# Three changes to the order of work in a two-block transformer kernel on one core: next weights in two parts around the norm's rows, first tile's rows between the second tile's heads, last unit's up product in one part

## Chip, cores and metric

One core of a Trainium2 chip runs the whole program. The metric is the device time of one execution in microseconds (us). In the tables PE is the matrix engine (PEld its weight loads), DVE the vector engine, ACT the scalar engine, POOL the GpSimd engine and SP the engine that issues most of the transfers (DMAs).

## What is computed

Two blocks of two layers each, on 256 tokens of width 1024 in fp32. The first block (token mixers and dense feed-forward layers) is not touched. Each layer of the second block is, in the reference:

```python
def second_block(x, positions, w_in, ..., expert_w_down, ln2_g, ln2_b):
    ...
    for l in range(DEPTH):                     # 2 layers
        mix = hybrid_mixer(x, tabs, w_in[l], mla_q_norm[l], mla_kv_norm[l], mla_w_uq[l], mla_w_ukv[l], w_o[l])
        x = layer_norm(DEEPNORM_ALPHA * x + mix, ln1_g[l], ln1_b[l])
        moe = hier_moe(x, router_group_w[l], ..., expert_w_gate[l], expert_w_up[l], expert_w_down[l])
        x = layer_norm(DEEPNORM_ALPHA * x + moe, ln2_g[l], ln2_b[l])
    return x
```

`hybrid_mixer` projects x by `w_in` into the inputs of three kinds of attention (the last is a dilated-window attention with four heads) and projects their outputs by `w_o`. `hier_moe` picks for each token a group of experts and two experts of its eight; there are 32 experts, each with `silu(x Wg) * (x Wu)` of width 256 and a product with `Wd`.

## The kernel before

The tokens are two tiles, t = 0 and 1, of 128 rows. A scheduler fixes one instruction order for each engine ahead of time; `tc.issue_after` and `tc.keep_in_program_order` steer it. An engine works through its own order, so an instruction that waits holds up all behind it. An fp32 product is three matmuls (`mm3`, L186): weights and data are each split into a high part, cast by ACT (`whi`, `x`, `yh`), and a low part, subtracted by DVE or POOL (`wlo`, `yl`).

**Splitting weights.** `raw_w` (L148) issues the load of a 4-chunk block into one of three `raw` buffers; `split_raw` (L158) casts it on ACT (L165) and subtracts on a given engine (L166), in four pieces. The mixer's first three projections of `w_in` have 416, 384 and 296 columns; the first has its weights loaded and split ahead, under the end of the layer before (`ahead`).

**Dilated heads, norm, router** (end of `mix2`, L950 on). `dil_pair` (L886) does scores on PE, the masked minimum on DVE (L901), exponentials on ACT (L906), scaling on DVE (`shares`, L650), transposes and the product with v on PE, then the split of the result (`x<-po`). Two pairs make one tile. `out_proj` (L945) multiplies by `w_o`; `rt.logits` (L1023) adds the residual (`raw`, L1027) and makes the router's logits; LayerNorm statistics follow; `rt.route` and `rt.place` pick experts and slots. `lows` (L1052) are the two low parts of a tile's normalised rows, 128x512 each. `nrm.affine` (L690, operations at L694) multiplies h by the norm's weight row and adds its bias row: four 128x512 operations a tile, eight in all. They come last, just ahead of the branch. The two rows lie in a buffer `rowb`, which is then loaded with expert weights.

**MoE.** The 32 experts go in eight units of four, 32 slots of tokens to an expert. `load` (L1175) issues 1 MB weight loads on SP into a ring of buffers. `gate_up` (L1235) does the gate product of a unit, then a branch on the token count (`most_i`, L1380 to L1386), then the up product; in the last unit (`parts=2`) the up product of its first three experts first, and of the fourth after it. DVE multiplies (`hq`, L1262), `hidden` transposes, `down` (L1272) multiplies by the down weights in column cuts, each split to `yh` (ACT, L244) and `yl` (DVE, L245); `spread` (L1295) sends the slots back to tokens.

**Between the layers.** `finish` (L1305) runs the last unit and then `nrm.finish` (L696): statistics, a square root by Newton steps on DVE (L258 to L272), two operations per half tile (L707, L708), after each of which `then` (L1474) transposes the new half for the next layer and splits it. Two weight blocks of the next layer (four chunks of 416 columns each) are split while this goes on, on POOL; so is the projection of 384 columns (`proj`, L767).

Of the kernel before, what the change touches and what calls it, by code (L numbers as in the profile page):

```python
# [8 lines left out]
F32 = mybir.dt.float32  # L9
# [8 lines left out]
NT = 2  # L18
# [9 lines left out]
CAP, NU = 32, NE // 4  # L28
MORE = 3
PIECES = 4  # L30

SPIN = 9

# [70 lines left out]
def tile_fn(ctx: ExitStack, tc: tile.TileContext, a: dict, out: bass.AP, stop=None, start=1):  # L104
# [538 lines left out]
    def exps(X, nm, sums):  # L643
        for t, (c0, c1) in enumerate(SPAN):
            nc.scalar.activation(X[:, c0:c1], X[:, c0:c1], AF.Exp, scale=-1.0, bias=nm[:, t:t + 1], accum_out=sums[:, t:t + 1])

    def shares(X, rs, PT):

        for r, c0, c1 in rs:
            nc.vector.tensor_scalar(X[:, c0:c1], X[:, c0:c1], r, None, op0=OP.mult)  # L650
        pt = ps.tile([128, 4, 128], F32, name="tp", tag="at", bufs=PB["at"])
        for b in range(3):
            nc.tensor.transpose(pt[:, b], X[:, b * 128:(b + 1) * 128], ident)
        PT = PT().rearrange("p (b c) -> p b c", b=3)
        nc.scalar.copy(PT, pt[:, :3])
        return PT
# [57 lines left out]
    def mix2(l, xp, wx, x, last, tabs, rt, ahead):  # L714
# [49 lines left out]
            kpe.append(kp)  # L764

        with tc.issue_after(last.ins) if last else nullcontext():
            acc = proj(x, w, 416, 384, eng=nc.gpsimd)  # L767
        for t in range(NT):
            kk = t384("bqk")
            nc.scalar.copy(kk[:, :320], acc[t][:, :320])  # L770
# [179 lines left out]
        nrm = LayerNorm("ln1", a["ln1_g_2"][l:l + 1, :], a["ln1_b_2"][l:l + 1, :])  # L950
        for t in range(NT):
            pair = [dil_pair(t, n) for n in range(2)]
            for n in (0, 1, 0, 1) if t == 0 else (0, 0, 1, 1):
                next(pair[n])
            for k in (0, 2, 4):
                for c in range(2):
                    out_proj(t, c, range(k, k + 2))
            if t:

                for low in lows:  # L960
                    low()
                rt.place(0)
            for c in range(2):
                out_proj(t, c, range(6, 8))
            raw = rt.logits(t, [acc[t, c] for c in range(2)])
            with tc.issue_after(rt.copied.ins):
                for c in range(2):
                    nrm.stat(t, c, raw[c])
            mv, y = nrm.stats(t)
            nb = nrm.shift(mv, y)  # L970
            with tc.issue_after(nrm.shifted.ins):
                rt.route(t, mv, y)

            lows = rt.features(t, raw, y, nb)
            if t == 0:
                rt.gates(t)
            else:
                lows[0]()
                rt.place(t)
                lows[1]()  # L980

        def affine():
            for t in range(NT):
                for c in range(2):
                    nrm.affine(t, c, nc.vector)
        return lambda: rt.gates(1), affine

    NR = 40

    class Route:  # L990
# [68 lines left out]
        def evacuate(self, xe, pg, k0, n):  # L1059

            for k in range(n):
                g, b = self.gx[:, 0, k0 + k:k0 + k + 1], self.gx[:, 1, k0 + k:k0 + k + 1]
                if k % 2:
                    nc.vector.tensor_scalar(xe[:, k0 + k], pg[:, k], g, b, op0=OP.mult, op1=OP.add)
                else:
                    nc.scalar.activation(xe[:, k0 + k], pg[:, k], AF.Identity, scale=g, bias=b)

# [94 lines left out]
    def moe(l, xp, wx, rt, then, ahead, rest):  # L1162
# [69 lines left out]
                for e, r in experts[i]:  # L1232
                    nc.vector.tensor_copy(gs[r, q:q + 1], pq[r, q, e:e + 1])

        def gate_up(i, xe, gs, between=None, after=None, parts=1, room=None):  # L1235

            units = list(enumerate(experts[i]))

            def product(m, us, pu):
                for k in range(8):  # L1240
                    for u, (_, r) in us:
                        nc.tensor.matmul(pu[r], xe[:, k, r], W[i][4 * m + u][:, k], start=k == 0, stop=k == 7, skip_group_check=True)  # L1242

            def new_pu():
                return ps.tile([128, 512], F32, name="at", tag="at", bufs=PB["at"])[:, :EH]
            hh, hq = room or (None, None)
            pu = new_pu()
            product(0, units, pu)
            if hh is None:
                hh = xp.tile([128, EH], F32, name="hh", tag="hh", bufs=1)  # L1250
            nc.scalar.activation(hh, pu, AF.Silu)
            if between:
                between()
            pu = new_pu()
            for us in (units,) if parts == 1 else (units[:3], units[3:]):
                product(1, us, pu)
            if after:
                after()
            if hq is None:
                hq = xp.tile([128, EH], F32, name="hq", tag="hq", bufs=1)  # L1260
            hq = hq.rearrange("s (k p) -> s k p", k=2)
            nc.vector.scalar_tensor_tensor(hq.rearrange("s k p -> s p k"), hh.rearrange("s (p k) -> s p k", k=2), gs,  # L1262
                                           pu.rearrange("s (p k) -> s p k", k=2), op0=OP.mult, op1=OP.mult)
            return hq
# [40 lines left out]
        def finish(i, PT, xe, gs, nrm, most):  # L1305

            acc = {}

            def start(c):

                for t in range(NT):
                    acc[t, c] = new_acc()
                    nc.tensor.matmul(acc[t, c], ident, h[t][:, c * 512:(c + 1) * 512], start=True, stop=False, skip_group_check=True)  # L1313
            hq = gate_up(i, xe, gs, lambda: rounds(i, most, CAP), lambda: start(0), parts=2)
            for n, (sl, y) in enumerate(down(i, hidden(hq), "at", cuts)):
                c, w = divmod(sl.start, 512)
                if n == 0:
                    start(1)
                for t in range(NT):
                    p = acc[t, c][:, w:w + sl.stop - sl.start]  # L1320
                    spread(p, PT, t, y, False)
                    nrm.stat(t, n, p)
            with tc.issue_after(done[0].ins):
                for k0 in ahead:
                    ahead[k0] = split_raw(ahead[k0], 4, 416, nc.gpsimd)
            nrm.finish([[acc[t, c] for c in range(2)] for t in range(NT)], then, l + 1 == DEPTH)

        def further(i, off):
# [43 lines left out]
        for i in range(NU):  # L1372
# [23 lines left out]
                finish(i, PT[:, q], xq, gq, nrm, most)  # L1396
            load(12 * (i + 1) + NB)
            if i == NU - 2:
                if l + 1 < DEPTH:
                    for k0 in (0, 4):  # L1400
                        ahead[k0] = raw_w(*block_w(a["w_in_2"][l + 1], k0, 4, 0, 416))
                nrm = LayerNorm("ln2", a["ln2_g_2"][l:l + 1, :], a["ln2_b_2"][l:l + 1, :], len(cuts), True)

    def store():
        for t in range(NT):
# [53 lines left out]
    for l in range(DEPTH):  # L1459
# [14 lines left out]
        def then(t, c):  # L1474
            sl = slice(c * 512, (c + 1) * 512)
            if l + 1 == DEPTH or stop == f"moe{l}":
                nc.sync.dma_start(out[0, t * 128:(t + 1) * 128, sl], h[t][:, sl])
            else:
                if c == 0:
                    nxt[t] = new_x(t)  # L1480
                r = split_t(h[t][:, sl], nxt[t], 4 * c, 4)
                if t == 0:
                    last.append(r)
        nxt, ahead = [None] * NT, {}
        with tc.tile_pool(name=f"moe{l}", bufs=1) as xp:
            moe(l, xp, wx, rt, then, ahead, rest)
# [32 lines left out]
```

## Time and profile before

| | |
|---|---|
| median of 3 runs | 1698.84 us (1697.95 to 1699.92) |
| the profiled execution | 1697.12 us |
| its span, first to last instruction | 1695.3 us |
| PE busy | 1560.3 us, 92% |
| DVE / ACT / POOL busy | 54% / 40% / 3% |
| mean granted PE clock | 0.952 of full speed |

The profiled execution is 1.7 us below the median and 1.8 us above its own span. The page shows busy shares over the whole span. Within it the dense parts keep PE busy without a gap, and the two MoE stretches (about 1050 to 1250 us and 1466 to 1672 us) keep the DMA engines busy at 414 to 419 GB/s while PE waits now and then.

### The profile page before, as it was taken

To read this page: it belongs to the slowest core of one execution; us is meant where nothing else is said; L and a number is where in the kernel's file an instruction comes from. 1 tells how busy PE (TensorE), PEld (TensorE's weight loads), DVE (VectorE), ACT (ScalarE), POOL (GpSimd) and SP (SyncE) were. 2 spreads that over 40 slices of the span, in tenths; PEclk is the share of its full clock that TensorE was granted. 3 is DMA by queue.
4 is the path that set the end of the run, shared out by engine and by line. 5 is a ranking of instruction groups with operands and counts; after the bars stand their busy time and mean duration, and the time that the engine had idled before them with its cause. 6 is when DMAs were issued, how large, how long until landed. Compare 5 with 4: busy or idle time off the path is not lost. (4 is left out here: it accounts for less than half of the span.)

```text
span 1695.3 us, 24281 instructions
## 1 busy us (share of the span) xinstructions
PE 1560.3 (92%) x9488; PEld 1183.4 (70%) x9488; DVE 909.1 (54%) x1990; ACT 679.5 (40%) x1118; POOL 58.2 (3%) x86
## 2 busy tenths in 40 slices
PE   9999999999999999999999998786679999877686
PEld 7788888888878888888887776442338777544353
DVE  6757576544675767555378656331147955522133
ACT  6543454443554345444356653110116655211011
POOL 0000000000000000000110100000011010000000
PEclk9999999999999999999999999897789999898699
DMA  9354555465635454646452728999985473899994
GB/s 326 125 176 163 172 198 194 154 200 197 210 124 174 154 192 153 198 161 211 155 162 78 286 108 318 419 418 419 418 311 162 130 259 134 332 418 418 419 415 164
DMA packets 133985, 399.36 MB, mean 236 GB/s; under 512 B 8133, under 2 KB 36805, under 8 KB 110278
## 3 DMA queue, kind: packets, MB, share of 16 engines
q1 hardware_dynamic: 130096, 390.62, 62.7%
q10 hardware_dynamic: 3734, 6.69, 1.1%
q8 instruction: 95, 1.56, 0.4%
q14 instruction: 60, 0.49, 0.1%
HBM read 396.24 MB, written 1.05 MB: 234 GB/s over the span
## 5 line engine op out<-in xcount | busy, mean ns | idle before, releaser
L166 DVE TENSOR_TENSOR wlo<-raw,whi 128x2048 fp32r<-128x2048 f32 (+6 forms) x314 | 405.8, 1310 | 305.2 <-ACT whi L165 304.6
L165 ACT CAST whi<-raw 128x2048 fp32r<-128x2048 f32 (+7 forms) x346 | 354.9, 1063 | 325.5 <-PE acc L192 273.8
L190 PE MATMUL acc<-whi,x 128*128 128x512 f32 (+3 forms) x1248 | 481.7, 387 | 0.1
L191 PE MATMUL acc<-wlo,x 128*128 128x512 f32 (+3 forms) x1248 | 477.2, 383 | 0.0
L192 PE MATMUL acc<-whi,x 128*128 128x512 f32 (+3 forms) x1248 | 476.3, 382 | 0.1
L190 PEld LDWEIGHTS acc<-whi,x 128*128 128x128 f32 x1248 | 236.9, 190 | 44.7 <-issue 3.5
L191 PEld LDWEIGHTS acc<-wlo,x 128*128 128x128 f32 x1248 | 237.0, 190 | 42.7 <-issue 2.7
L192 PEld LDWEIGHTS acc<-whi,x 128*128 128x128 f32 x1248 | 236.5, 190 | 42.5 <-issue 1.4
L1242 PE MATMUL at<-whi,xe 128*32 128x256 f32 x448 | 101.1, 434 | 21.3 <-DMA whi<-in_expert_w_gate_dram 15.0
L1242 PE MATMUL at<-wlo,xe 128*32 128x256 f32 x416 | 85.7, 442 | 17.4 <-DVEq L1386 8.8
L1262 DVE SCALAR_TENSOR_TENSOR hq<-hh,gs,at 128x256 f32<-128x256 f32 x16 | 10.5, 657 | 140.6 <-PEq L1391 92.6
L1242 PE MATMUL at<-wx,xe 128*32 128x256 f32 x416 | 57.0, 421 | 17.0 <-DMA wx<-in_expert_w_gate_dram 8.1
L245 DVE TENSOR_TENSOR yl<-acc,yh 128x512 fp32r<-128x512 f32 x30 | 20.6, 688 | 96.9 <-ACT yh L244 96.9
L166 POOL TENSOR_TENSOR wlo<-raw,whi 128x416 fp32r<-128x416 f32 (+1 forms) x32 | 32.9, 1064 | 1129.9 <-ACT whi L165 1129.9
L191 PE MATMUL acc<-wlo,fh 128*128 128x512 f32 x176 | 70.0, 398 | 0.0
L190 PE MATMUL acc<-whi,fh 128*128 128x512 f32 x176 | 69.9, 397 | 0.0
L192 PE MATMUL acc<-whi,fl 128*128 128x512 f32 x176 | 69.9, 397 | 0.0
L1275 ACT COPY hT<-ph 128x256 f32<-128x256 f32 x17 | 6.3, 373 | 144.2 <-PE ph L1269 135.3
L1242 PE MATMUL at<-more,xe 128*32 128x256 f32 x352 | 53.8, 432 | 10.8 <-PEq L1386 7.6
L1242 PEld LDWEIGHTS at<-wlo,xe 128*32 128x32 f32 x416 | 36.7, 125 | 38.8 <-issue 25.9
L1242 PEld LDWEIGHTS at<-whi,xe 128*32 128x32 f32 x448 | 42.5, 123 | 30.4 <-issue 18.2
L1242 PE MATMUL at<-raw,xe 128*32 128x256 f32 x320 | 49.1, 435 | 9.6 <-PEq L1386 3.9
(385 smaller groups left out, 2166.7 us busy)
## 6 DMA issues: line engine op xcount, KB each, us to landing
raw<-in_w_in_dram SPq DMA_DIRECT2D x55, 1024.0 KB, 5.1
raw<-in_w_gate_up_dram SPq DMA_DIRECT2D x40, 1024.0 KB, 5.2
raw<-in_w_down_dram SPq DMA_DIRECT2D x22, 1024.0 KB, 4.9
whi<-in_expert_w_gate_dram SPq DMA_DIRECT2D x16, 1024.0 KB, 13.9
raw<-in_w_in_dram SPq DMA_DIRECT2D x28, 512.0 KB, 4.2
wx<-in_expert_w_up_dram SPq DMA_DIRECT2D x14, 1024.0 KB, 19.0
wx<-in_expert_w_down_dram SPq DMA_DIRECT2D x14, 1024.0 KB, 7.1
wlo<-in_expert_w_up_dram SPq DMA_DIRECT2D x14, 1024.0 KB, 17.1
```

The costliest lines, as they stand in the source:

```text
L165: nc.scalar.copy(hi[:, s], raw[:, s])
L166: eng.tensor_tensor(lo[:, s], raw[:, s], hi[:, s].bitcast(F32), op=OP.subtract)
L190: nc.tensor.matmul(acc, xhi[:, kt], whi[:, k, c0:c1], start=first, stop=False)
L191: nc.tensor.matmul(acc, xhi[:, kt], wlo[:, k, c0:c1], start=False, stop=False)
L192: nc.tensor.matmul(acc, xlo[:, kt], whi[:, k, c0:c1], start=False, stop=last)
L245: nc.vector.tensor_tensor(lo, p, hi.bitcast(F32), op=OP.subtract)
L1242: nc.tensor.matmul(pu[r], xe[:, k, r], W[i][4 * m + u][:, k], start=k == 0, stop=k == 7, skip_group_check=True)
L1262: nc.vector.scalar_tensor_tensor(hq.rearrange("s k p -> s p k"), hh.rearrange("s (p k) -> s p k", k=2), gs, pu.rearrange("s (p k) -> s p k ...
L1275: nc.scalar.copy(hT, ph)
```

## The change

Three parts. In the router part of each of the two layers, tile 0's low parts and the four operations on its norm rows are issued between and after the second tile's heads; tile 1's four stay at the end, after the expert inputs are evacuated. In the last unit of each layer the up product of all four experts is one loop. Between the two layers, the first weight block is split with DVE and the second, on POOL, only after the first transposed half of tile 0; 22 matmuls without use (`SPIN_LN`) are put ahead of the norm; the norm's row loads stand between the two weight loads; and the projection of 384 columns uses DVE in layer 1.

```diff
     def shares(X, rs, PT):
         for r, c0, c1 in rs:
-            nc.vector.tensor_scalar(X[:, c0:c1], X[:, c0:c1], r, None, op0=OP.mult)
+            share[0] = nc.vector.tensor_scalar(X[:, c0:c1], X[:, c0:c1], r, None, op0=OP.mult)
...
-            acc = proj(x, w, 416, 384, eng=nc.gpsimd)
+            acc = proj(x, w, 416, 384, eng=nc.vector if l else nc.gpsimd)
...
-            for n in (0, 1, 0, 1) if t == 0 else (0, 0, 1, 1):
+            for m, n in enumerate((0, 1, 0, 1) if t == 0 else (0, 0, 1, 1)):
                 next(pair[n])
+                if t and m % 2:
+                    with tc.issue_after(share[0].ins):
+                        for c in range(2):
+                            lows[c]() if n == 0 else nrm.affine(0, c, nc.vector)
...
             if t:
-                for low in lows:
-                    low()
                 rt.place(0)
...
         def affine():
-            for t in range(NT):
+            with tc.issue_after(rt.evacuated.ins):
                 for c in range(2):
-                    nrm.affine(t, c, nc.vector)
-        return lambda: rt.gates(1), affine
+                    nrm.affine(1, c, nc.vector)
+        return affine, lambda: rt.gates(1)
...
-            for us in (units,) if parts == 1 else (units[:3], units[3:]):
-                product(1, us, pu)
+            product(1, units, pu)
...
             for n, (sl, y) in enumerate(down(i, hidden(hq), "at", cuts)):
                 c, w = divmod(sl.start, 512)
+                if n == 0 and ahead:
+                    with tc.issue_after(done[0].ins):
+                        ahead[0] = split_raw(ahead[0], 4, 416, nc.vector)
...
-            with tc.issue_after(done[0].ins):
-                for k0 in ahead:
-                    ahead[k0] = split_raw(ahead[k0], 4, 416, nc.gpsimd)
+            if ahead:
+                idle = ps.tile([128, 512], F32, name="po", tag="po", bufs=PB["po"])[:, :128]
+                for _ in range(SPIN_LN):
+                    tc.keep_in_program_order(nc.tensor.matmul(idle, ident, ident, start=True, stop=True))
             nrm.finish([[acc[t, c] for c in range(2)] for t in range(NT)], then, l + 1 == DEPTH)
...
-                if l + 1 < DEPTH:
-                    for k0 in (0, 4):
+                for k0 in (0, 4):
+                    if l + 1 < DEPTH:
                         ahead[k0] = raw_w(*block_w(a["w_in_2"][l + 1], k0, 4, 0, 416))
-                nrm = LayerNorm("ln2", ...)
+                    if k0 == 0:
+                        nrm = LayerNorm("ln2", ...)
...
                 if t == 0:
                     last.append(r)
+                    if c == 0:
+                        with tc.issue_after(r.ins):
+                            ahead[4] = split_raw(ahead[4], 4, 416, nc.gpsimd)
```

The order of DVE in the router part of layer 0, before, from the split of the second tile's last heads (`x<-po`) on (`h_70` is tile 0, `h_71` tile 1):

```order
L245 TENSOR_TENSOR x_7735<-po,x_7735 128x128
L1052 TENSOR_TENSOR x_8004<-h_70,x_8004 128x8x64 x2
L1146 SCALAR_TENSOR_TENSOR rk_8231<-sg_8000,rk 128x32
L1027 SCALAR_TENSOR_TENSOR raw<-h_71,acc 128x512
L1130 TENSOR_TENSOR P<-tabstrict,rk_8231 128x128 x2
L1027 SCALAR_TENSOR_TENSOR raw<-h_71,acc 128x512
L676 BN_STATS lst<-raw 128x6 x2
```

And in the changed kernel, whose lines stand up to 18 lower (L698 is the old L694, L1034 the old L1027):

```order
L1153 SCALAR_TENSOR_TENSOR rk_8235<-sg_8000,rk 128x32
L1137 TENSOR_TENSOR P<-tabstrict,rk_8235 128x128 x2
L247 TENSOR_TENSOR x_7735<-po,x_7735 128x128
L698 TENSOR_TENSOR h_70<-h_70,rowb 128x512
L1034 SCALAR_TENSOR_TENSOR raw<-h_71,acc 128x512
L698 TENSOR_TENSOR h_70<-h_70,rowb 128x512 x2
L1034 SCALAR_TENSOR_TENSOR raw<-h_71,acc 128x512
L698 TENSOR_TENSOR h_70<-h_70,rowb 128x512
L680 BN_STATS lst<-raw 128x6 x2
```

Tile 0's four row operations now stand around the two residual sums; its two low parts went further up, ahead of the masked minima of the last heads:

```order
L247 TENSOR_TENSOR x_7735<-po,x_7735 128x128
L1059 TENSOR_TENSOR x_8004<-h_70,x_8004 128x8x64 x2
L905 ISA smx,dnm<-at,tabcm 128x384
L905 ISA dnm 128x1
```

There the first row is the split of the first pair, and L905 is the old L901; before, L901 followed at once. On PE seven `out_proj` matmuls follow the last product with v, where fourteen did, since the scheduler put more of them among the heads.

The order of ACT at the end of layer 0, before, from the down product's casts on:

```order
L244 CAST yh<-at 128x512 x2
L165 CAST whi<-raw 128x416 x4
L133 DMA tabcm<-in_tab_dram 128x1024
L996 DMA rw<-in_router_w_dram 128x320
L165 CAST whi<-raw 128x416 x4
```

And in the changed kernel (L246 is the old L244, L167 the old L165):

```order
L246 CAST yh<-at 128x512
L167 CAST whi<-raw 128x416 x4
L246 CAST yh<-at 128x512
...
L246 CAST x_12733<-tp 128x512
L167 CAST whi<-raw 128x416 x4
L246 CAST x_12733<-tp 128x512
```

The casts of the first weight block moved ahead of the second `yh`; those of the second block now wait behind the first cast of transposed data (`x<-tp`). DVE has its four subtractions of the first block between the first `yl` and the first statistics.

## Rows read from the trace of the kernel before

**Rows 1.** Windows: us, each engine's busy time, granted PE clock, DMA share, GB/s.
```profile
1055.00:1100.00 45.00, 35.38 (x360) 20.78 (x352) 15.06 (x42) 7.04 (x14) 0.00 (x0) 0.92 1.01 419
1262.00:1275.00 13.00, 4.92 (x19) 4.42 (x20) 12.36 (x25) 5.15 (x12) 7.25 (x8) 0.61 0.93 323
1290.00:1436.00 146.00, 144.64 (x848) 117.17 (x848) 97.39 (x355) 90.44 (x233) 11.29 (x24) 0.96 0.47 162
```
**Rows 2.** Timeline of SP: start, us of the issue; layer 0, then layer 1.
```profile
1050.00 0.33 SPq L1186 DMA_DIRECT2D rowb<-in_expert_w_up_dram  x1
...
1466.05 0.33 SPq L1186 DMA_DIRECT2D rowb<-in_expert_w_up_dram  x1
```
**Rows 3.** Timeline of DVE, router part of layer 0: start, us, operation, [idle before].
```profile
1019.84 0.56 DVE L901 CUSTOM_DVE_ANT_1 smx<-at,tabcm 128x384 f32<-128x384 f32 x1
...
1028.03 0.29 DVE L245 TENSOR_TENSOR x<-po,x 128x128 fp32r<-128x128 f32 x1 [3.04 <-ACT x L244]
1028.24 2.22 DVE L1052 TENSOR_TENSOR x<-h,x 128x512 fp32r<-128x512 f32 x2
...
1031.47 0.68 DVE L1027 SCALAR_TENSOR_TENSOR raw<-h,acc 128x512 f32<-128x512 f32 x1
...
1044.58 5.39 DVE L694 TENSOR_TENSOR h<-h,rowb 128x512 f32<-128x512 f32 x8
```
**Rows 4.** Timeline of PE, the out_proj matmuls after the second tile's heads.
```profile
1030.49 0.39 PE L190 MATMUL acc<-whi,x 128*128 128x512 f32 x1
1030.72 0.39 PE L191 MATMUL acc<-wlo,x 128*128 128x512 f32 x1
```
**Rows 5.** Windows of line 1242 alone, the last up product of layers 0 and 1.
```profile
1242.00:1248.30 6.30, 6.26 (x64) 3.29 (x64) 1.00 1.05 384
1665.50:1671.90 6.40, 6.27 (x64) 3.29 (x64) 1.00 0.59 217
```
**Rows 6.** Timeline of PE, two steps of the last gate product, four experts side by side.
```profile
1239.67 0.38 PE L1242 MATMUL at<-whi,xe 128*32 128x256 f32 x1
...
1239.88 0.38 PE L1242 MATMUL at<-whi,xe 128*32 128x256 f32 x1
```
**Rows 7.** Tile raw, 1240 to 1264 us: its issues on SP and their landing.
```profile
L152 SPq DMA_DIRECT2D raw<-in_w_in_dram x3: 379/531/612, 1242.7 to 1259.7; - x3
...
DMA to landing us min/median/max: 4.7/11.0/12.1
```
**Rows 8.** Timeline of ACT and POOL, the weight blocks of 416 columns.
```profile
1258.74 1.86 ACT L165 CAST whi<-raw 128x416 fp32r<-128x416 f32 x4
...
1259.36 8.29 POOL L166 TENSOR_TENSOR wlo<-raw,whi 128x416 fp32r<-128x416 f32 x8 [281.86 <-ACT whi L165]
```
**Rows 9.** Timeline of DVE at the end of layer 0.
```profile
1258.87 0.69 DVE L245 TENSOR_TENSOR yl<-at,yh 128x512 fp32r<-128x512 f32 x1 [1.44 <-ACT yh L244]
...
1261.37 0.33 DVE L680 BATCH_NORM_AGGREGATE lmv<-lst 128x2 f32<-128x12 f32 x2
...
1262.17 1.34 DVE L268 SCALAR_TENSOR_TENSOR rs_q<-rs_y,lv 128x1 f32<-128x1 f32 x2
...
1268.03 0.75 DVE L707 SCALAR_TENSOR_TENSOR acc<-acc,lmv,rowb 128x512 f32<-128x512 f32 x1
```
**Rows 10.** Timeline of DVE at the end of layer 1, the same chain.
```profile
1684.99 0.35 DVE L680 BATCH_NORM_AGGREGATE lmv<-lst 128x2 f32<-128x18 f32 x2
...
1687.38 0.75 DVE L707 SCALAR_TENSOR_TENSOR acc<-acc,lmv,rowb 128x512 f32<-128x512 f32 x1
```
**Rows 11.** Timeline of PE between the layers: first transposes, those of cq, first matmul of 384 columns.
```profile
1269.72 1.09 PE L239 MATMUL tp<-tabident,h 128*128 128x128 f32 x4 [9.37 <-DVE h L708]
...
1284.02 0.52 PE L239 MATMUL tp<-tabident,cq 128*128 128x128 f32 x3 [0.82 <-DVE cq L757]
1284.30 0.42 PE L190 MATMUL acc<-whi,x 128*128 128x384 f32 x1
```
**Rows 12.** Timeline of PE, matmuls that only keep PE busy, in the router part.
```profile
1034.45 2.25 PE L1140 MATMUL rk<-tabident 128*128 128x128 f32 x18
```

More of the change, by code (lines that the diff above doesn't have):

```diff
@@ L30 @@
 PIECES = 4
+SPIN_LN = 22
 SPIN = 9
@@ L645, in exps @@
             nc.scalar.activation(X[:, c0:c1], X[:, c0:c1], AF.Exp, scale=-1.0, bias=nm[:, t:t + 1], accum_out=sums[:, t:t + 1])
+    share = [None]
     def shares(X, rs, PT):
         for r, c0, c1 in rs:
-            nc.vector.tensor_scalar(X[:, c0:c1], X[:, c0:c1], r, None, op0=OP.mult)
+            share[0] = nc.vector.tensor_scalar(X[:, c0:c1], X[:, c0:c1], r, None, op0=OP.mult)
         pt = ps.tile([128, 4, 128], F32, name="tp", tag="at", bufs=PB["at"])
@@ L1063, in evacuate @@
                 if k % 2:
-                    nc.vector.tensor_scalar(xe[:, k0 + k], pg[:, k], g, b, op0=OP.mult, op1=OP.add)
+                    self.evacuated = nc.vector.tensor_scalar(xe[:, k0 + k], pg[:, k], g, b, op0=OP.mult, op1=OP.add)
                 else:
@@ L1233, in slots, with gate_up @@
                     nc.vector.tensor_copy(gs[r, q:q + 1], pq[r, q, e:e + 1])
-        def gate_up(i, xe, gs, between=None, after=None, parts=1, room=None):
+        def gate_up(i, xe, gs, between=None, after=None, room=None):
             units = list(enumerate(experts[i]))
@@ L1313, in start @@
                     nc.tensor.matmul(acc[t, c], ident, h[t][:, c * 512:(c + 1) * 512], start=True, stop=False, skip_group_check=True)
-            hq = gate_up(i, xe, gs, lambda: rounds(i, most, CAP), lambda: start(0), parts=2)
+            hq = gate_up(i, xe, gs, lambda: rounds(i, most, CAP), lambda: start(0))
             for n, (sl, y) in enumerate(down(i, hidden(hq), "at", cuts)):
                 c, w = divmod(sl.start, 512)
+                if n == 0 and ahead:
+                    with tc.issue_after(done[0].ins):
+                        ahead[0] = split_raw(ahead[0], 4, 416, nc.vector)
                 if n == 0:
@@ L1398, in moe @@
             if i == NU - 2:
-                if l + 1 < DEPTH:
-                    for k0 in (0, 4):
+                for k0 in (0, 4):
+                    if l + 1 < DEPTH:
                         ahead[k0] = raw_w(*block_w(a["w_in_2"][l + 1], k0, 4, 0, 416))
-                nrm = LayerNorm("ln2", a["ln2_g_2"][l:l + 1, :], a["ln2_b_2"][l:l + 1, :], len(cuts), True)
+                    if k0 == 0:
+                        nrm = LayerNorm("ln2", a["ln2_g_2"][l:l + 1, :], a["ln2_b_2"][l:l + 1, :], len(cuts), True)
     def store():
```

## The prediction

> **What bounds the kernel now.** I read the windows first. In the MoE stretch the DMA engines are full (share 1.01, 419 GB/s) while PE is busy 35.38 of 45 us; in the mixer that follows between the layers PE is busy 144.64 of 146 us, and the 13 us between those two are neither: PE busy 4.92 us, at a granted clock of 0.61 [rows 1]. So three kinds of rule hold. In the MoE a microsecond counts where it moves the start of the weight stream, or comes after its last load. Between the layers it counts where it brings PE's projections forward, since after them PE has no gap to lose it in. Elsewhere it counts little.
>
> The start of the stream: SP issues a load into `rowb`, the norm's two rows' buffer, at 1050.00 in layer 0 and at 1466.05 in layer 1 [rows 2]. In layer 0 that is when DVE ends the eight row operations, 1044.58 + 5.39 = 1049.97 [rows 3]. So DVE's chain through the router, and these operations at its end, set the stream's start. A step on that chain is paid in full.
>
> **Part A: tile 0's rows among the second tile's heads (both layers).** Taken away at the end: four of eight operations of 5.39 / 8 = 0.67 us, so 2.70 us [rows 3]. Added earlier, on the same chain:
> - The two low parts, 2.22 us, stood behind `x<-po` at 1028.24; now they stand ahead of the masked minima at 1019.84. The minima then start 2.2 us later, and as the first combining step now stands behind three of them and not two, the exponentials start another 0.56 us later [rows 3]. From there to `x<-po` every step waits for the one before (DVE sits idle 3.04 us for ACT ahead of it [rows 3]), so `x<-po` goes from 1028.03 to about 1030.8.
> - There DVE no longer has 2.2 us of low parts, and only seven `out_proj` matmuls follow instead of fourteen, at 0.23 us each [rows 4]: the sums are ready from about 1032.0. But DVE does one row operation (0.67) ahead of the first residual sum, two between the sums and one behind the second. The second sum stood at 1031.47 to 1032.15 [rows 3]; I get 1034.0 to 1034.7, and the statistics 0.6 later still, about 3.1 us late in all.
>
> Net +3.1 - 2.7 = **+0.4 us a layer**. Bounds: if the rows between the sums fill time in which the sums are not ready, +1.8 and so a gain of about 1 us; if nothing overlaps, 2.22 + 0.56 + 2.70 - 2.70, or +2.8. I take +0.4, as I have walked the order row by row; it lies nearer the low end because the seven `out_proj` matmuls that went ahead give back 1.6 us.
>
> **Part B: the up product of the last unit in one loop (both layers).** The two parts take 6.26 and 6.27 us at full clock [rows 5]. Four experts side by side advance one step in 1239.88 - 1239.67 = 0.21 us [rows 6]; fifteen more steps and the last matmul (0.38) make 3.5 to 3.6 us. Saved: **2.65 us** in the chain that ends in `hq`.
> - Layer 1: nothing follows but `hq`, down, spread, norm and output, each waiting for the one before. All of it is kept: -2.65. It would be less, down to 0, if the fourth expert's up weights were late; PE has none of the waiting in this product that would show that.
> - Layer 0: ACT now has the four casts of the first weight block ahead of the second `yh`. That block's load is issued at 1242.7 and lands at most 12.1 us later, at 1254.8 [rows 7]. So however early `hq` is, the casts (1.86 us [rows 8]) end near 1256.7, DVE's four subtractions (by its 512-wide operations at 0.67, about 0.57 each) near 1257.6, and two statistics later the second `yl` ends near 1259.4, where it ended at 1259.56 [rows 9]. Kept: 0.15 us of 2.65. Bounds: 0 and -2.65.
>
> **Part C: weights in two parts, between the layers.** The Newton steps behind the statistics take from 1261.37 to 1268.03, 6.66 us, in layer 0, and 1684.99 to 1687.38, 2.39 us, in layer 1 [rows 9, 10]. The difference is POOL, which subtracts from 1259.36 on for 8.29 us [rows 8]; two steps of L268, on one element a partition, alone take 1.34 us [rows 9]. The change leaves POOL idle there: -4.3, with the 0.15 above, and PE's first transposes, at 1269.72 now [rows 11], come near 1265.6 if A moves the stream by 0.4 and nothing else moves.
>
> [...]
>
> The 22 spare matmuls, at 2.25 / 18 = 0.125 us a record and 0.25 a matmul (an fp32 matmul of 9 leaves 18 records) [rows 12], take about 5.5 us behind the last spread matmul. That one stands between the second `yl` (1259.56) and the aggregation (1261.37) [rows 9]; from 1260.4 they end at 1265.9, just about when the transposes can start: 0 to 0.6 us of delay. With them PE stays at the full clock that it has in the last unit (1.00 [rows 5]); in the gap it was granted 0.61 [rows 1], and four transposes took 1.09 us [rows 11].
>
> From the first transposes to the 384 projection there are 14.58 us now (1269.72 to 1284.30 [rows 11]). Their last part is a wait of PE for `cq`, 0.82 us, and its transposes [rows 11], which the change puts behind the projection. I count anew: 0.55 for the first transposes at full clock, a cast and a subtraction of about 0.6 and 0.69 [rows 9], 48 matmuls of 416 columns at 0.23 x 416 / 512 = 0.19 [rows 4], and 0.6 for transposes in between: 11.4 us. The projection then starts near 1277, some 7.4 us early. One set of transposes moved behind it costs 0.3. From there PE is full [rows 1], and the gain holds: **-7.1 us**, part A's 0.4 of layer 0 already in it. Bounds: -4 (no gain from clock or `cq`) to -9.7 (part B's layer-0 gain kept too).
>
> Twelve DVE pieces are new (four of 416, eight of 384), eight of them in the mixer of layer 1, with about 0.57 us each. They stand beside 11 us of PE work on the two tiles and beside the norm's eight operations and four `yl`-like splits, 7 us of their own. DVE has room, barely.
>
> **Sum.** -7.1 (layer 0: C with A and B) + 0.4 (A, layer 1) - 2.65 (B, layer 1) = -9.35. The profiled execution took 1697.12 us, so 1687.8; the median of the runs shown is 1.72 above it, so **1689.5 us**. A measurement of this kernel can tell about 0.2%, 3.4 us, from no change.
>
> **Rivals.**
> 1. *Part A is not paid back.* The interleaved rows stand in DVE's order ahead of what the router waits for; at +2.8 instead of +0.4 a layer: +4.8, 1694.3. For it: DVE works in order. Against: DVE waits 3 us twice among the heads. Chance 0.15.
> 2. *More is kept.* If the first weight block lands earlier, since the stream starts earlier in part A (-1 a layer), or the casts don't hold up the second `yh`, up to 2.65 + 2.8 more: 1684 to 1686. Against: the landing row. Chance 0.15.
> 3. *Slower: PE loses its clock in the router.* With the minima 2.8 us later, PE waits among the second tile's heads without the seven `out_proj` matmuls left to fill it. PE's clock does fall in a gap: 0.61 in the 13 us where it had 4.92 us of work [rows 1]. If it falls here, some 13 us of PE work in the chain to the expert inputs takes twice as long, of which I count half as waited for: +6.4 a layer. -9.35 + 12.8 is +3.5, 1702.3. It decides from a gap like the one between the layers; the gaps I expect are 2 to 3 us, so the chance is 0.05.
> 4. *The weights land later.* If the row loads, now between the two weight loads, delay either of them by their 1 MB (2.5 us at 419 GB/s [rows 1]), the second block's casts come behind: 1692. Chance 0.1.
> [...]
>
> That the change doesn't do what it says is out: the order of the instructions shows each part.
>
> **How the numbers follow.** My forecast keeps 0.4, and its own range is 1687 to 1692. With rivals 1, 2, 4 and 5 the range is 1684 to 1696; rival 3 and the far ends of 1 are left out. Faster by over 0.2% means below 1695.4: all of the forecast, 2, 4 and 5, and half of 1, with some room for errors that I have not named: 0.83. Within 0.2%: 0.12. Slower: 0.05.
>
> **What would show it.** A: the `rowb` load near 1050.4 and 1466.5 minus what layer 0 gained; `x<-po` of the last heads near 1030.8. B: 64 records of the last up product in about 3.6 us, `hq` some 2.6 us earlier. C: the chain from L680 to L707 near 2.4 us, the first transposes near 1265.6 at 0.6 us for four, the 384 projection near 1277. The forecast is wrong if the granted clock between 1020 and 1042 drops, if the transposes wait for the spare matmuls, or if a wait of PE for a subtraction or a cast appears between 1266 and 1290.

## The result and the profile after

The changed kernel takes 1709.02 us (median of 5 runs, 1706.74 to 1714.9) where the kernel before takes 1698.84 beside it: **ratio 1.007, 95% interval 1.0056 to 1.0084, slower**. The forecast was 1689.5, in 1684 to 1696.

The profiled execution took 1710.69 us (span 1708.9), 13.57 more than that of before. Some 2.7 of it is there ahead of any changed instruction: a load into `wlo` that SP issues at 1012.24 before stands at 1014.92. So I compare distances between fixed points, in us:

| stage | before | after | |
|---|---|---|---|
| `rowb` load, layer 0, to the first transposes | 219.72 | 217.47 | -2.25 |
| first transposes to `rowb` load, layer 1 | 196.33 | 195.78 | -0.55 |
| `rowb` load to the extra round of layer 1 | 135.30 | 136.21 | +0.91 |
| extra round to the last `hq` | 70.60 | 83.74 | **+13.14** |
| last `hq` to the end | 23.39 | 23.39 | 0 |

(The extra round, L1214 before and L1221 after, is where unit 5 of layer 1 serves tokens beyond 32 slots.) The gain between the layers is there, smaller than forecast; one stage, where the change only shortens a product, loses 13 us. PE's waits there, in total us, times and longest, in the kernel after (1595 to 1690):

```profile
PE at L1221 <- DVE oP L1137: 5.5, 1, 5.5
PE at L1249 <- PEq L1367: 4.7, 1, 4.7
PE at L1221 <- issue: 3.8, 1, 3.8
PE at L1249 <- PEq L1398: 3.6, 1, 3.6
...
```

The first of these is in the kernel before too (5.2 us there), and it is put down to DVE, but DVE itself waits there for a branch of PE, which takes 5.83 us before (L1355) and 6.06 after (L1367). The other three are new, and none names another engine: PEq is PE's own sequencer, "issue" a stop that nothing in the profile releases. L1398 is the branch on the count `most_i` in unit 6, L1367 that in the last unit (L1386 and L1355 before). The view of one line shows the branch (ns min/median/max), first after:

```profile
L1398 PEldq COMPARE_BRANCH  x1: 4248/4248/4248, 1652.4 to 1652.4; - x1
...
L1367 PEldq COMPARE_BRANCH  x1: 5557/5557/5557, 1674.0 to 1674.0; - x1
```

then before:

```profile
L1386 PEldq COMPARE_BRANCH  x1: 374/374/374, 1647.3 to 1647.3; - x1
...
L1355 PEldq COMPARE_BRANCH  x1: 366/366/366, 1663.6 to 1663.6; - x1
```

The same two instructions take 9.1 us more. With the issue stop that is 12.9. The up products behind them then run on a PE that has been idle. In the windows, the columns being length, busy time (instructions) of PE, PEld, DVE, ACT, POOL, granted clock, DMA share, GB/s, first the whole stage before, after, and in all_w, the whole change with PE's code at its old length (told of below):

```profile
1601.35:1671.95 70.60, 64.06 (x657) 38.43 (x658) 18.96 (x44) 10.37 (x22) 0.00 (x0) 0.90 0.98 387
1601.75:1685.49 83.74, 66.78 (x657) 40.07 (x658) 18.95 (x43) 10.35 (x22) 0.00 (x0) 0.82 0.84 328
1604.24:1672.08 67.84, 61.36 (x657) 37.12 (x658) 18.95 (x43) 10.35 (x22) 0.00 (x0) 0.90 1.01 399
```

then the two branches of after:

```profile
1652.00:1657.00 5.00, 1.45 (x28) 0.63 (x20) 0.00 (x0) 0.38 (x1) 0.00 (x0) 0.86 0.54 218
1657.00:1666.00 9.00, 7.93 (x80) 4.07 (x84) 0.65 (x1) 0.37 (x1) 0.00 (x0) 0.70 0.75 265
1666.00:1673.00 7.00, 7.00 (x60) 3.06 (x56) 3.20 (x6) 1.17 (x2) 0.00 (x0) 1.00 0.94 301
1673.00:1680.00 7.00, 2.31 (x46) 1.17 (x39) 0.66 (x2) 0.38 (x1) 0.00 (x0) 0.97 0.76 266
1680.00:1686.00 6.00, 6.00 (x66) 3.73 (x67) 0.51 (x1) 0.00 (x0) 0.00 (x0) 0.76 0.02 5
```

PE does 1.45 us of work in the 5 us of the first branch, then is granted 0.70 over 9 us (0.50 from 1655.8 to 1662.5, 1.00 from 1662.7 to 1666); likewise 0.76 behind the second (0.50 from 1679.7 to 1682.9, then 1.00). The kernel before has 1.00 in all its windows from 1645 to 1672. By an estimate from these two windows, at 0.70 and 0.76 their 15 us hold about 9 x 0.30 + 6 x 0.24 = 4 us that full clock would not need. Over the whole stage the sum can be read from its three rows. PE's idle time goes from 6.54 us before to 16.96 after, 10.4 more; that is less than the 12.9, since PE still works off earlier matmuls while a branch runs. Its busy time is 61.36 in all_w, 2.7 less than before by part B, and 66.78 after: 5.4 more for the same matmuls at a lower clock. So 10.4 of idle time and 5.4 of clock, less the 2.7 of part B, make the 13.1 us.

What does PE do in a branch of 5 us? The DMA view has two queues of the kind "instruction"; over the whole execution the larger, q8, moves 97 packets of some 16 KB, one in 18 us. In the 5.6 us of the last unit's branch alone (packets, MB, share of 16 engines):

```profile
q8 instruction: 1, 0.02, 1.2%
q14 instruction: 2, 0.02, 0.8%
```

The unit 6 branch of after also has one q8 packet within it, and so has the issue stop (1603.08 to 1606.90); in the same two branches of before, q8 has none. Over the last 36 to 40 us of the MoE both kernels move the same, 4 packets of q8 and 4 of q14. That q8 brings PE's code I take from where PE runs straight, ahead of its first branch. Before, from 22.00 to 963.11, in the columns of the windows and of the queues above:

```profile
22.00:963.11 941.11, 935.51 (x4553) 764.43 (x4552) 579.28 (x986) 450.52 (x588) 21.87 (x29) 0.99 0.53 177
q8 instruction: 36, 0.59, 0.3%
```

That is a packet of 16 KB for every 253 matmuls and weight loads of PE. In all the profiles of this document it is 254 to 255, when PE's semaphore records are counted with them. So I take it that PE's program is being loaded piece by piece, and that in one kernel a piece comes in the branch, in the other at some other time. That is my theory, **PE waits for its own code**. What the change added to PE's code are the 22 spare matmuls, 44 records of 9532, and as many weight loads; parts A and B add none. Rivals: it is their time or PE's clock, not their number (theory 2); part A costs it (theory 3).

### The profile page after: what moved, and what is told of

Read it like the earlier page. It is cut to its first block, busy times and chain, and to the rows that moved or that the text cites. A ratio compares the mean times of both kernels' runs of the same rounds, so it can differ in the third digit from the quotient of the medians.

```text
span 1708.9 us, 24357 instructions
## 1 busy us (share of the span) xinstructions
PE 1566.1 (92%) x9532; PEld 1184.9 (69%) x9532; DVE 906.8 (53%) x2002; ACT 678.8 (40%) x1118; POOL 46.6 (3%) x74
## 3 DMA queue, kind: packets, MB, share of 16 engines
q8 instruction: 97, 1.59, 0.4%
## 5 line engine op out<-in xcount | busy, mean ns | idle before, releaser
L168 DVE TENSOR_TENSOR wlo<-raw,whi 128x2048 fp32r<-128x2048 f32 (+7 forms) x326 | 412.3, 1282 | 310.8 <-ACT whi L167 309.7
L167 ACT CAST whi<-raw 128x2048 fp32r<-128x2048 f32 (+7 forms) x346 | 355.2, 1063 | 328.8 <-PE acc L194 273.0
L1249 PE MATMUL at<-wlo,xe 128*32 128x256 f32 x416 | 82.6, 422 | 17.6 <-PEq L1367 4.7
L1268 DVE SCALAR_TENSOR_TENSOR hq<-hh,gs,at 128x256 f32<-128x256 f32 x16 | 10.5, 657 | 142.3 <-PEq L1403 113.2
L246 ACT CAST yh<-acc 128x512 fp32r<-128x512 f32 x30 | 17.6, 586 | 98.9 <-PE acc L1288 98.9
```

The lines of the kernel that those rows point to most:

```text
L167: nc.scalar.copy(hi[:, s], raw[:, s])
L168: eng.tensor_tensor(lo[:, s], raw[:, s], hi[:, s].bitcast(F32), op=OP.subtract)
L246: r = nc.scalar.copy(hi, p)
```

## Experiments

### The parts alone

```diff
# a_only: part A's hunks; b_only: part B's; c_only: part C's; ab: A and B
+                            lows[c]() if n == 0 else nrm.affine(0, c, nc.vector)   # A
-            for us in (units,) if parts == 1 else (units[:3], units[3:]):           # B
+SPIN_LN = 22                                                                        # C
```

> Part A alone, in both layers. Code theory: the lost time comes from two compare-and-branch steps of PE in layer 1 (units 6 and 7, 4.25 and 5.56 us instead of 0.37) and a stop of 3.8 us in the extra rounds before them, all of them waits for PE's own code, and only part C's 22 matmuls move PE's code ahead of them. Then both branches are short here (under 0.5 us) and the time is that of before within 2 us. Phase theory (the code waits because it competes with the weight stream, and any shift of the stream can do it): one or both may be long, 1702 to 1709. Stream theory (A delays the stream): +0.5 to +3 us a layer, to be read from the load into rowb.

> Part B alone, in both layers. Code theory: branches of units 6 and 7 in layer 1 under 0.5 us, time 2 to 3 us below before (2.65 us from layer 1). Weight theory (the last up product now waits for the fourth expert's weights and its branch with it): the last up product of layer 1 starts some 4 us late, time 1 to 3 us above before. Phase theory: 1696 to 1707.

> Part C alone. Code theory: at least one of the branches of units 6 and 7 in layer 1 takes over 3 us, and the stop in the extra rounds is there, as in the whole change; the mixer between the layers gains 3 to 4 us, so the time is 5 to 9 us above before. Phase theory: the stream of layer 1 starts 3 to 4 us early, any pattern. If the loss is due to A or B: 3 to 4 us below before.

> Parts A and B without C. Code theory: branches of units 6 and 7 in layer 1 under 0.5 us, time 1 to 4 us below before. Phase theory: as in the whole change, 1702 to 1707. If C's gain and the loss are unrelated and the loss is A's and B's: about 10 us above before plus C's missing 4, 1712.

Measured, beside 1697.49 for before: A 1700.18, ratio 1.0018 (1.0006 to 1.0029); B 1693.52, 0.9975 (0.9965 to 0.9985); C 1707.97, 1.0064 (1.0046 to 1.0082); A and B 1693.34, 0.9982 (0.9968 to 0.9997). The loss is in part C, although C changes nothing in layer 1's MoE; it is 10.5 us, more than the 5 to 9 expected. There, c_only has the same two long branches, and b_only does not:

```profile
L1394 PEldq COMPARE_BRANCH  x1: 3488/3488/3488, 1647.7 to 1647.7; - x1
...
L1363 PEldq COMPARE_BRANCH  x1: 5479/5479/5479, 1667.6 to 1667.6; - x1
```

### The spare matmuls taken out, and put in alone

```diff
# spin0: the whole change, with
-SPIN_LN = 22
+SPIN_LN = 0
# spin_only: the kernel before, with
+                for _ in range(SPIN_LN):      # 22, ahead of nrm.finish
+                    tc.keep_in_program_order(nc.tensor.matmul(idle, ident, ident, start=True, stop=True))
```

> The whole change without the 22 spare matmuls, all else as in it. Code theory: PE's code ahead of layer 1's MoE is as long as before, so the branches of units 0 to 4 of layer 1 are long again (2 to 5 us, hidden under the stream) and those of units 6 and 7 short (0.37 us); time 8 to 12 us below the whole change, about 1698. Phase theory (the time at which layer 1's stream runs decides, which the split of the weights moves): units 6 and 7 stay long, time within 3 us of the whole change.

> The kernel before with the 22 spare matmuls and nothing else. They stand where PE waits 9.4 us for the norm, so they hold up nothing, and PE keeps its clock over the gap (a gain of 1 to 2 us). Code theory: the branches of units 6 and 7 in layer 1 take over 3 us each and the time is 6 to 10 us above before. Phase theory: the stream of layer 1 hardly moves, branches as before, time 0 to 2 us below before.

Measured, beside 1696.87: spin0 1693.94, ratio 0.9993 (0.9976 to 1.001), branches 0.37 and 0.36 us; spin_only 1710.7, 1.0082 (1.0065 to 1.0099):

```profile
L1393 PEldq COMPARE_BRANCH  x1: 3608/3608/3608, 1654.7 to 1654.7; - x1
...
L1362 PEldq COMPARE_BRANCH  x1: 4466/4466/4466, 1673.0 to 1673.0; - x1
```

Twenty-two matmuls that nothing waits for in layer 1, put between the layers, reproduce the whole loss: +13.8 us (6 to 10 were expected), 400 us ahead of where it appears. The issue stop in the extra round is there as well, 3.84 us in spin_only and 3.83 in c_only, each with one q8 packet. Theory 3 is out as its main cause. (spin0's ten times fall in two groups, 1691.3 to 1694.9 and 1699.9 to 1700.5; its profile is of the first, and what the second holds wasn't seen.)

### Fewer of them, without part A

```diff
# bc8, bc16, bc0: parts B and C, with
+SPIN_LN = 8        # 16, 0
```

> Parts B and C with 8 spare matmuls and without A. Code theory: the pattern of long branches in layer 1 is one of its own, between those of 0 and 22; if units 6 and 7 are short, the time is 5 to 8 us below before (B 4, C 3 to 4 less the clock that 8 matmuls don't hold); if they are long, it is near before. Phase theory: as with 22 matmuls, 1703.

> Parts B and C with 16 spare matmuls and without A. Code theory: a pattern of its own again; short at units 6 and 7: 6 to 9 us below before; long: near before or up to 5 us above. Phase theory: as with 22 matmuls, 1703.

> Parts B and C without spare matmuls and without A; the control for the next run. Code theory: branches of units 6 and 7 in layer 1 short, as in before. B gives 4 us less than before by its own run; C gives from 0 (its gain between the layers is lost to a wait of ACT) to 3 us: 1690 to 1693.

Measured: 8 give 1699.04, ratio 1.0013 (1.0004 to 1.0023); 16 give 1702.68, 1.003 (1.002 to 1.004); both beside 1696.87. None gives 1694.31, 0.9979 (0.9965 to 0.9992), beside 1697.07. All branches of PE's two last units, by profiles of one execution each:

| kernel | PE records | branch of unit 6, us | of the last unit, us |
|---|---|---|---|
| before, a_only, b_only, ab, spin0, bc0, a_late, all_w, bcw, best2 | 9488 | 0.37 | 0.36 to 0.37 |
| bc8 | 9504 | 4.65 | 0.37 |
| bc16 | 9520 | 3.77 | 0.36 |
| spin_only, c_only, after | 9532 | 3.61, 3.49, 4.25 | 4.47, 5.48, 5.56 |
| bc0_lg, best | 9488, and two loads by POOL | 4.98, 4.91 | 0.36, 0.37 |

(The last four names of the first row, and the last row, are told of below.) Every long one in the table has one q8 packet that begins within it, and no short one has. Over the 17 profiles PE takes 561 branches: of the 149 that last over 2.5 us each has such a packet, of the 358 under 1 us six have, and of the 54 between one has. The time of the spare work, from 0 to 7.2 us (bcw), does not order the table; the length of PE's code does. Compiled from the kernels of the runs, it is 32002 to 32004 instructions in the first row, 32027 in the last, 32035 with 8 spare matmuls, 32067 with 16, and 32090 or 32091 with 22. Nor does the start of layer 1's stream order it: with the `rowb` load at 1462.61 (bcw), 1466.05 (before) and 1468.14 (ab) the branches are short, at 1463.19 (c_only), 1465.54 (after) and 1469.13 (spin_only) long, so the phase theory is out. Why a certain length leads to a stop and another to none, no run shows.

### One load moved to POOL's queue, and wide spare matmuls

```diff
# bc0_lg: bc0, with
-            nc.scalar.dma_start(lg[:, :256], a[...
+            nc.gpsimd.dma_start(lg[:, :256], a[...      # both halves of lg
# best: bc0_lg, with
-                for _ in range(SPIN):                    # in rank, 9 of 128 columns
+                for n in range(6):                       # two of 384, four of 128
...
-                for _ in range(SPIN_LN):
-                    ...matmul(idle, ident, ident, start=True, stop=True))
+                for _ in range(SPIN_LN):                 # 4, and 2 ahead of the last spread
+                    ...matmul(idle, ident, xe[:, :4], start=True, stop=True))   # 512 columns
```

> The run before, with the two loads of the mixer's norm rows (lg, 128 and 64 KB) issued by POOL instead of ACT. Theory: in the whole change and in C alone ACT can't issue the first of them until the table's load has landed (1267.75, issue at 1267.77 in C alone), and its first cast of transposed data stands behind both; so PE waits 2.9 us there. Without them on ACT that wait of PE falls to under 1 us, and the first 384-column matmul comes 1 to 2.5 us earlier after the first transposes than in the control; 1 to 2 us less in all. Rival (the cast waits for the transposes or the clock, not for the loads): no change in that distance.

> B and C with lg on POOL, and PE kept busy by 6 matmuls of 512 columns (2 ahead of the last spread, 4 behind it) in place of 22 of 128; in each router 9 matmuls of 128 columns become 2 of 384 and 4 of 128, so that PE's code ahead of layer 1's MoE is as long as before. Code theory: branches of units 6 and 7 in layer 1 short; with PE's clock held over the norm, 1 to 3 us below the run before: 1687 to 1691. If it is the spare time on PE and not the length of its code that makes the branches long, they are long here too, and the time is 1698 to 1705.

In after, ACT's first cast for the next layer stands behind two loads of `lg` that ACT issues at 1270.31, and PE waits 1.51 us for it. With the loads on POOL that wait is gone in bc0_lg, the way from the first transposes to the projection falls from 16.05 us in bc0 to 14.07, as expected, and yet: bc0_lg 1698.45, ratio 1.0007 (0.9998 to 1.0017); best 1696.59, 0.9998 (0.9988 to 1.0008). Both have the long branch in unit 6, with as many PE records as before; bc0_lg has no spare work at all, so it is not that which makes the branch of best long, against what I expected of best. In the compiled program, PE's code has waits on two more semaphores at the ends of loops and branches, those of the two loads that POOL issues: 24 instructions more than in bc0 with no matmul more.

### The whole change at the old length of PE's code

```diff
# all_w: the whole change, with the wide spare matmuls of best, lg on ACT
# bcw: all_w without part A
# best2: bcw, with the router's loads behind the copy that they delay
```

> The whole change with PE's code kept as long as before ahead of layer 1's MoE: 6 spare matmuls of 512 columns in place of 22 of 128 columns, and in each router 2 of 384 and 4 of 128 in place of 9 of 128. Code theory: branches of units 6 and 7 in layer 1 under 0.5 us each, the last up product of layer 1 within 68 us of the extra round's first matmul (83.7 in the whole change), time 12 to 15 us below the whole change, 1694 to 1697. Rival (spare matmuls on PE, of whatever length, push PE's code loading): branches long, within 4 us of the whole change.

> The run above without part A. Code theory: both branches short; A costs 1 to 1.5 us a layer, so 2 to 3 us below the run above, 1691 to 1694. The run called best differed in the loads of lg by POOL alone; if those (their waits in the loops' ends make PE's code longer) made its unit 6 long, it is short here.

> The run above, with the router's five small loads of each layer issued after the first two tiles' part of the mixer, so that ACT's loads ahead of the first cast are three and not eight. Theory of the loads: PE's wait at the first 416-column matmul falls from 1 to 3 us to under 1, and it is 0 to 2 us below the run above: 1689 to 1693. Rival (nothing waits for them): the same.

Measured, beside 1697.46: all_w **1694.58, ratio 0.9979 (0.9967 to 0.9991)**, bcw **1689.28, 0.9953 (0.994 to 0.9965)**, best2 1693.31, 0.9967 (0.9956 to 0.9978). all_w is the whole change with spare work of about the same time in as many records as before has: short branches, and 14 us less than after. That settles theory 2. bcw is better than both kernels. It is also below its own forecast. Delaying the router's loads brought nothing (the median is 4 us above that of bcw, the intervals overlap): PE's wait at the first 416-column matmul was already down to 0.68 us in bcw, and a wait of 2.04 us for `cq` came up.

### Part A: the order of SP

```diff
# a_late: part A alone, with
-        load(NB)
+        load(NB - 1)
         for i in range(NU):
...
+            load(NB)          # the raw load behind it follows the read of the count
```

> Part A with the load into rowb put behind the first read of the token count, where it stood before the change; A alone was 3 us slower than before. Theory (SP waits with the load into rowb for DVE's last row operation, and only then reads the count and issues the next loads, 2 us late): the next loads are issued within 0.6 us of the load into rowb again, and the time is 1 to 3 us below A alone, near before. Rival (A's cost is DVE's longer chain in the router): no change from A alone.

Measured: 1697.88 beside 1697.07, ratio 1.001 (0.9996 to 1.0024). That is 2.3 us below A alone, as forecast, but the two intervals overlap, and it did not come about as forecast: the `raw` load, which I wanted earlier, stays at 1052.38. What holds it shows in a_only; on SP, in layer 0:

```profile
1049.95 0.33 SPq L1191 DMA_DIRECT2D rowb<-in_expert_w_up_dram  x1
1052.49 0.33 SPq L1191 DMA_DIRECT2D raw<-in_expert_w_up_dram  x1
```

and the first branch of layer 0's MoE on PE:

```profile
L1391 PEldq COMPARE_BRANCH  x1: 4037/4037/4037, 1048.3 to 1048.3; - x1
...
L1391 PEldq EVENT_SEMAPHORE  x1: 51/51/51, 1052.4 to 1052.4; - x1
```

The `rowb` load goes out when DVE is done; the next ones go out with the end of PE's branch at 1052.4, and the profile names PE's sequencer at L1391 as what SP waited for. In the kernel before this branch already takes 4.2 us, and it also has a q8 packet within it:

```profile
L1386 PEldq COMPARE_BRANCH  x1: 4202/4202/4202, 1045.4 to 1045.4; - x1
```

It ends at 1049.6, by chance with DVE's rows, at 1049.97 [rows 3]. Part A puts PE's entry to it 3 us later, and nothing shortens it. A variant of A without this branch's 4 us was not tried.

## Why the prediction was wrong

**The step that failed** is the price of the 22 spare matmuls: "about 5.5 us behind the last spread matmul ... 0 to 0.6 us of delay". I priced their time, where they stand. What they cost is their place in PE's code: two branches and a stop, from the extra round of unit 5 in layer 1 on, that take 12.9 us more and leave PE idle for 10.4 more, and 5.4 us of clock behind these. No term and no rival had that. What the traces show of the cause is that q8 brings 16 KB (1.59 MB in 97 packets) for every 253 of PE's records where PE runs straight, and that each branch over 2.5 us has such a packet beginning in it; what the runs show is that 44 matmul records and 44 weight loads put ahead of layer 1's MoE change which of its branches are long. By what rule a branch becomes long no run here shows. The nearest was rival 3, PE at half clock in the router (0.50 is what the four transposes between the layers had before, from 1269.72 to 1270.81), where the windows of after show 1.00 (1020 to 1042, PE busy 19.86 of 22). Without the extra code the whole change (all_w) gives -0.21%, the sign that I forecast and some 3 of my 9.35 us. Its profile, the slowest of its eight executions, has 5.06 us of part C at the projection of 384 columns (229.24 us from the `rowb` load of layer 0, 234.30 before) and 2.7 of part B, but of the 5.06 only 0.45 is left at the `rowb` load of layer 1, where bcw keeps 6.45. So the step "From there PE is full [rows 1], and the gain holds" did not hold in it either: PE ran the mixer between at a granted clock of 0.94, against 0.96 before and 0.97 in bcw.

That long branches exist was there to read in the kernel before. In layer 1, units 0 to 4:

```profile
L1386 PEldq COMPARE_BRANCH  x5: 2249/3699/4730, 1461.2 to 1560.0; - x5
```

and after:

```profile
L1398 PEldq COMPARE_BRANCH  x5: 340/349/1521, 1463.7 to 1561.1; - x5
```

The change made these shorter, and nothing came of it: there PE waits for the weight stream anyway. From 1470 to 1600 the DMA share is 1.01, at 418 GB/s, in both kernels, and PE is busy 95.70 us before and 95.88 after; its waits for its own branch at L1386 (L1398 after) fall from 12.6 us to none, and those for loads rise from 10.7 to 17.6. Behind the extra round none of PE's waits, in either kernel, is for a load any more, and there the stops moved to.

**Part A, +0.4 a layer.** In plain times the statistics came 2.97 us late in a_only (forecast 3.1), and the `rowb` load 0.05 early (forecast 0.4 late); but a_only was 1.54 us ahead by the statistics of tile 0, which A does not touch, and from there to the load PE was granted 0.93 of its clock, where before has 0.99. After, with 1.00, is the cleaner row: from tile 0's statistics to tile 1's it takes 31.67 us (29.01 before), so 2.66 late, and to the `rowb` load 46.54 (46.94 before), so 0.40 early. The walk along DVE's order was right to within a microsecond. Wrong was "that is when DVE ends the eight row operations", that DVE alone sets the start: two chains ended there together, and I saw only the one that the profile named. The 4.55 us that PE sat idle ahead of the MoE stand in it as a wait for DVE's branch at L1386; PE's own branch at the same line lasts 4.2 us and covers some 3.4 of them. In a_only the loads of the steady stream go out 1.5 to 1.7 us later in layer 0 and about 1.2 in layer 1 (plain times), between the 0.4 that I took and the 2.8 of rival 1. In whole times A costs 2.7 us alone and nearly nothing with B. Between all_w and bcw it is 5.3; in their profiles that lies in the mixer of layer 1, whose length from the first transposes to the `rowb` load varies from 194 to 201 us over all the profiles. In bcw, then in all_w:

```profile
1268.56:1462.61 194.05, 186.97 (x1163) 153.26 (x1161) 139.97 (x497) 117.89 (x300) 15.52 (x28) 0.97 0.55 192
1268.15:1467.90 199.75, 193.92 (x1162) 158.56 (x1162) 140.18 (x497) 117.66 (x300) 15.44 (x28) 0.94 0.53 187
```

The same matmuls take PE 7 us longer at the lower granted clock, so these 5.3 us are not all A's. What makes the clock fall there no run shows.

**Part B, -2.65 in layer 1, 0.15 kept in layer 0.** Right in layer 1: in b_only the stage to the last `hq` goes from 70.60 to 67.71, and what follows is the same. In layer 0, b_only keeps 2.2 (219.72 to 217.51) when C does not stand behind it: the casts that I had hold up the second `yh` are not there in b_only, since only C moves them forward. With C they do hold it, as forecast.

**Part C, -7.1.** In after the chain from aggregation to the first norm operation is what I forecast, 2.17 us for 2.4, now that POOL is idle beside it (its first piece starts at 1272.34). The timeline of DVE there (start us, us, engine, line, operation, out<-in):

```profile
1264.41 0.33 DVE L684 BATCH_NORM_AGGREGATE lmv<-lst 128x2 f32<-128x12 f32 x2
...
1266.58 0.75 DVE L711 SCALAR_TENSOR_TENSOR acc<-acc,lmv,rowb 128x512 f32<-128x512 f32 x1
1267.37 0.75 DVE L712 SCALAR_TENSOR_TENSOR h<-acc,rs_y,rowb 128x512 f32<-128x512 f32 x1
```

And that of PE, with the idle time ahead and its releaser in brackets:

```profile
1260.53 0.73 PE L1301 MATMUL acc<-yh,PT 128*128 128x512 f32 x2 [1.82 <-ACT yh L246]
1262.66 0.88 PE L1301 MATMUL acc<-yl,PT 128*128 128x512 f32 x2 [1.40 <-DVE yl L247]
1263.34 6.59 PE L1337 MATMUL po<-tabident 128*128 128x128 f32 x44
1269.76 0.60 PE L241 MATMUL tp<-tabident,h 128*128 128x128 f32 x4
1271.88 0.46 PE L192 MATMUL acc<-whi,x 128*128 128x416 f32 x1 [1.51 <-ACT x L246]
```

The half `h` is ready at 1268.12; the transposes come at 1269.76, because the spare matmuls run until then. They take 6.6 us and not 5.5: PE idles 1.82 and 1.40 us ahead of them, waiting for the second `yh` and `yl`, and the granted clock from 1262.7 to 1269 is 0.73 (in c_only and spin_only they take 5.1). Then 1.51 us for a cast that stands behind ACT's loads. So the transposes are 1.5 us later than my 1265.6 (on a scale without the 2.68 of the start), and the way to the 384-column projection (1282.41) takes 12.65 us where I counted 11.4 (14.58 before [rows 11]). The projection is 4.6 us early, not 7.4, and of that a wait of 1.83 us for `cq` at 1292 takes part. The mechanism was right and the size too large, by spare work in the way and one queue that I didn't walk. bcw shows the size: the stage shrinks to 215.55 and the way to the projection to 11.80,

```profile
1263.49 5.23 PE L1337 MATMUL po<-xe,tabident 128*128 128x512 f32 x8
1268.56 0.60 PE L241 MATMUL tp<-tabident,h 128*128 128x128 f32 x4
...
1280.36 0.33 PE L192 MATMUL acc<-whi,x 128*128 128x384 f32 x1
```

with 219.72 + 14.58 before, so 6.95 us less from the `rowb` load to the projection, near the forecast 7.1.

**Rivals 2 and 4** were not seen: no more was kept than the terms above, and after the first block's casts, which begin with its landing at 1258.14 (1255.5 on the scale of before, forecast 1254.8), ACT waits for no load of the second block.

**Rival 5**, which the forecast's range and chances count in, was that POOL's four pieces hold up DVE's subtractions and make DVE the bound between the layers. No run shows that term. Taking POOL away shortened the chain of tiny operations from 6.66 [rows 9] to 2.17 us. Beside DVE's 384-column subtractions POOL hardly ran: one of them ran beside it in after, with 0.57 us, and one in c_only, with 0.55, where the others took 0.54 to 0.55. There the piece of POOL beside it took 1.41 and 1.39 us instead of 1.08 to 1.10, so it was POOL's piece that got longer, and whether DVE would be held up behind POOL no run here shows.

## What to carry to other kernels

Price an instruction that is added to an engine's program twice: by its time where it stands, and by the shift that it gives to all the code behind it (here 22 matmuls that nothing waits for cost 13.8 us in spin_only); read the durations of the branches of that engine (not only its busy time) in every stage where it is the bound. If spare work is wanted on PE, a few wide matmuls do what many narrow ones do and leave the code its length: here 9488 records of PE in all_w against 9532 in after, and 14 us between the two. When an engine sits idle ahead of a branch, look at its own branch before believing the engine that the profile names: here PE's took 4.2 us where DVE's was named.

## What was not expected of the hardware

A compare-and-branch on PE took 0.36 to 0.37 us or 3.5 to 5.6 us at the same place of the program, depending on how many instructions stand hundreds of microseconds ahead of it, and each long one had an instruction packet of 16 KB beginning within it. The branches of ACT, SP, DVE and POOL at the same lines took 0.037 to 0.072 us. Two loads issued by POOL in place of ACT brought the long branch back (4.98 us in bc0_lg) with no matmul added. Whether the code could be laid out so that its long branches never stand where PE is the bound stays open.
